# Thirty numbers in a list scheduler: new prices for matmuls, scans, strided views, half-array products, shape changes and hops between engines

## The chip, the cores and the metric

The kernel runs on one core of one Trainium2 chip. The metric is device time in microseconds (us) of one execution. The engines of the core are PE (TensorE, with PEld for its weight loads), DVE (VectorE), ACT (ScalarE), POOL (GpSimd) and SP (SyncE, which issues nearly all DMAs here).

## The reference

One layer of a hybrid decoder serves 2064 prompt tokens (16 of them learned meta tokens) and 64 sample tokens, 2128 columns in all. Cut to what matters:

```
q, k, v, u = split(rms_norm(x, g_mix) @ w_in)           # 1024 -> 512 | 128 | 128 | 512
o_att = sliding-window attention with sinks (8 query heads on 2 kv heads, window 128)
xr, xi = u_group @ Bbar                                 # 32 groups of 16 channels, 64 complex states each
h[t] = Lambda_bar * h[t-1] + x[t]                       # a scan over positions
y = Re(C h) + D u;  g = gelu(y);  o_ssm = g * sigmoid(g @ w_glu + b)
h = x + concat(rms_norm(o_att), rms_norm(o_ssm)) @ w_out
out = h + (silu(f @ w_gate) * (f @ w_up)) @ w_down,  f = rms_norm(h), 1024 -> 2816 -> 1024
```

It also returns the last 128 keys and values and the final scan states.

## The kernel before

All work is fp32. Large products are made from three products of fp32r halves (`mm3`), and the FFN uses a seven-product scheme on quarter matrices, so that the FFN is some 8300 matmuls of 352 columns. The program has five stages: `phase_u` (the projection to u, tiles `pu`, results `us` stored to `uD`), `phase_prep` (parameters of the scan), `phase_mix` (attention tiles of 128 tokens beside 16 scan steps of two channel groups each), `phase_out` (tiles `po`, after `out_weights` has split the output weights) and `phase_ffn` (tiles `ga`, `gb`, `gc`, `da`, `db`).

In `phase_mix` an attention tile is: `qkv_k` (48 matmuls into `pa`), `qk_sq`, `qk_n` (tile `qn`), `qkT`, `scores` (into `ps`, with the row maximum `mx` by a custom DVE instruction), exponentials on ACT, `p_t`, `p_v`. A scan step is: `ssm_x` (a product into `px`, then `xt` and `xs` on DVE), `ssm_add`, `ssm_scan` (two scans into `gg`), `ssm_rot` (`xt`, `xs` again), `ssm_h` (writes `hc`), `ssm_y` (products of `it` and of `mo` with `hc` into `yp`), `ssm_g`, `ssm_z` (a product into `px` again).

No line of these functions sets the order of the program. Every operation is recorded by `Plan.note` with its dependencies and with a price in ns from `Plan.price`. `Plan.issue` then plays a list schedule: each engine has a free time, an operation becomes ready when its producers have ended, plus a `hop` that depends on the two engines, and among the ready operations of an engine the one with the longest `tail` (priced work behind it, plus a bias per stage) goes next. PSUM banks are handed out in the same play. The operations are then emitted in the order of their played start times. Each engine runs its own instructions strictly in that order, and waits on semaphores for other engines' results and for its own earlier results. So a price has no effect on any instruction's duration; it decides what stands before what on each engine, and which bank a product uses.

Since every instruction is emitted by the recorder, all of them carry one source line in the profile (L279); tiles tell them apart.

Of the kernel before, what the change touches and what calls it, by code (L numbers as in the profile page):

```python
# [9 lines left out]
F32R = mybir.dt.float32r  # L10
# [160 lines left out]

class Op:
    __slots__ = ("eng", "cost", "wait", "call", "deps", "order", "next", "succ", "tail", "left", "ready", "start", "n", "set", "tiles",
                 "into", "part", "dma", "port")


class Plan:
# [18 lines left out]
    def turn(self, old, *new):  # L196

        pools = [LazyPool(self, *p) for p in new]

        def call():  # L200
            for p in [p for p in reversed(self.open) if p in old]:
                p.ctx.close()
                self.open.remove(p)
            for p in pools:
                p.ctx = ExitStack()
                p.got = p.ctx.enter_context(self.tc.tile_pool(name=p.name, bufs=p.bufs, side=p.side))
                self.open.append(p)

        if not old:
            call()  # L210
            return pools
        g = Op()
        g.eng, g.n, g.cost, g.wait, g.set, g.tiles, g.into = "gate", len(self.ops), 0, 0, None, [], None
        g.part = None
        g.order, g.dma, g.port = set(), False, False
        g.deps = set().union(*[p.ops for p in old])
        for p in old:
            p.over = True
        for p in pools:
            p.gate = g.n  # L220
        g.call = call
        self.ops.append(g)
        return pools

    def note(self, eng, name, args, kw):
        o = Op()
        o.eng, o.n, o.part = eng, len(self.ops), self.part
        vals = list(args) + list(kw.values())
        outs = [v for k, v in kw.items() if k in ("out", "accum_out")]
        if "out" not in kw:  # L230
            outs.append(args[0])
        outs = [v for v in outs if isinstance(v, Lazy)]
        ins = [v for v in vals if isinstance(v, Lazy) and not any(v is w for w in outs)]
        deps, order = set(), set()
        use = [(v.base, v.region(), False) for v in ins] + [(v.base, v.region(), True) for v in outs]
        for t, r, w in use:
            assert not t.over and not t.pool.over, t.kw
            if t.first is None:
                if t.pool.gate is not None:
                    deps.add(t.pool.gate)  # L240
                if t.before is not None:
                    t.before.over = True
                    deps.update(n for n, _ in t.before.reads + t.before.writes)
                if t.prev is not None and t.prev.first is not None:
                    order.add(t.prev.first)
            else:
                order.add(t.first)
            for n, rr in t.writes:
                if rr & r:
                    deps.add(n)  # L250
            if w:
# [12 lines left out]
        deps.discard(o.n)  # L264
        o.deps, o.order = deps, order - deps - {o.n}
        o.dma = "dma" in name
        o.cost, o.wait = self.price(eng, name, args, kw)
        o.port = self.ported(eng, name, outs, args, kw)
        fn = args[2] if eng == "scalar" and name == "activation" else None
        o.set = {AF.Sin: "sin", AF.Silu: "silu", AF.Exp: "exp", AF.Tanh: "exp"}.get(fn)  # L270

        bases = o.tiles = list({id(v.base): v.base for v in vals if isinstance(v, Lazy)}.values())
        o.into = next((v.base for v in outs if v.base.psum), None)
        for t in bases:
            t.count += 1

        def call():
            f = lambda v: v.real() if isinstance(v, Lazy) else v
            getattr(getattr(self.nc, eng), name)(*[f(v) for v in args], **{k: f(v) for k, v in kw.items()})  # L279
            for t in bases:  # L280
                t.count -= 1
                if not t.count:
                    t.got = None

        o.call = call
        self.ops.append(o)

    part, BIAS = None, {"prep": 3e3, "att": 6e3, **{"ssm%d" % i: 2e3 * (i - 4) for i in range(5, 17)}}

    HOP = {("tensor", "scalar"): 200, ("tensor", "vector"): 200, ("tensor", "gpsimd"): 225,  # L290
           ("vector", "tensor"): 256, ("vector", "scalar"): 200, ("vector", "gpsimd"): 205,
           ("scalar", "tensor"): 281, ("scalar", "vector"): 142, ("scalar", "gpsimd"): 170,
           ("gpsimd", "tensor"): 135, ("gpsimd", "vector"): 74, ("gpsimd", "scalar"): 75,
           ("tensor", "tensor"): 0, ("vector", "vector"): 127, ("scalar", "scalar"): 150, ("gpsimd", "gpsimd"): 102}

    def hop(self, a, b):
        if "gate" in (a, b):
            return 0
        if b == "sync":
            return 1250  # L300
        return 1100 if a == "sync" else self.HOP[a, b]

    PORT = False

    def ported(self, eng, name, outs, args, kw):

# [9 lines left out]
    def price(self, eng, name, args, kw):  # L316

        psum = lambda v: isinstance(v, Lazy) and v.base.psum
        out = kw.get("out", args[0] if args else None)
        n = int(np.prod(out.shape[1:]))  # L320
        ap = lambda v: isinstance(v, (Lazy, bass.AP))
        if "dma" in name:
            return 100 + out.shape[0] * n * 4 / (370 if out.shape[-1] >= 128 else 190), 1000
        if eng == "tensor":
            if name == "transpose":
                return 0.85 * args[1].shape[0], 0
            return (0.417 * n if args[1].dtype == F32R else 1.68 * max(n, 64)) + 3, 0
        if eng == "scalar":
            c = 0.83 * n + (60 if psum(args[1]) else 95) + 90 * ap(kw.get("bias")) + 90 * ap(kw.get("scale")) + 90 * ("accum_out" in kw)
            return c, 0  # L330
        if eng == "vector":
            if name == "tensor_reduce":
                return 1.04 * int(np.prod(args[1].shape[1:])) + 70, 0
            fast = name in ("tensor_copy", "tensor_scalar", "memset") and not psum(args[1] if len(args) > 1 else None)
            c = 65 + 65 * (name in ("tensor_scalar", "scalar_tensor_tensor") and ap(args[2]))
            return (3 if name == "reciprocal" else 0.52 if fast else 1.04) * n + c, 0
        if kw.get("op") == ALU.pow:
            return 165 * n + 300, 0
        return {"tensor_scalar": 1.37, "memset": 0.8, "tensor_copy": 1.0}.get(name, 2.15) * n + 135, 0

    def issue(self):
# [28 lines left out]
        banks = [(0.0, "b%d" % i) for i in range(8)]  # L370
        whole = {b: False for _, b in banks}
        left = {t: t.count for o in ops for t in o.tiles if t.psum}
        order, table, pipe, port = [], None, 0.0, 0.0
        for _ in ops:
            get = [min((b for b in banks if whole[b[1]] or not y), default=(1e12,)) for y in (False, True)]
            at = lambda o: (max(o.ready, get[o.into.seeded][0], 1e12 * bool(need.get(o.into))) if o.into and "tag" not in o.into.kw
                            else max(o.ready, port) if o.port and self.PORT else o.ready)
            free["sync"] = max(free["sync"], pipe)
            t, e = min((max(free[e], min(map(at, row))), e) for e, row in cand.items() if row)
            o = max((o for o in cand[e] if at(o) <= t), key=lambda o: o.tail)  # L380
# [10 lines left out]
            end = t + o.cost  # L391
            if o.dma:
                pipe = end = max(t + 2000 * (e == "gpsimd"), pipe) + o.cost
            if o.set is not None and o.set != table:
                end += 1283
                table = o.set
            free[e] = t + 1340 if o.dma and e == "gpsimd" else end
            if o.port:
                port = end
# [1378 lines left out]
```

## Time and profile before

| | |
|---|---|
| median of 3 runs | 2150.8 us (2147.27 to 2153.14) |
| profiled execution, its own time | 2150.36 us |
| span of the profile, first to last instruction | 2148.5 us |
| busy PE, DVE, ACT, POOL | 2049.7, 1735.1, 1295.8, 101.6 us |
| granted TensorE clock, mean | 0.977 of full speed |
| instructions | 35113 |

By the trace, the u projection ends on PE at about 148 us, the mix of attention and scan steps runs to about 570 us with output work beginning in it at 558 us, the output projection ends at about 785 us, and the rest is the FFN. Busy times of PE count the modelled end of each pipelined matmul, so they overstate; a matmul's cost in a dense stretch is read from the distance between starts.

### The profile page before, as it was taken

What the parts mean: (1) busy time and instruction counts of PE and PEld (TensorE: products, weight loads), DVE (VectorE), ACT (ScalarE), POOL (GpSimd) and SP (SyncE); (2) the same over time, 40 slices, a digit from 0 to 9 for tenths busy, and PEclk for the clock granted to TensorE, in tenths of its full rate; (3) what the DMA queues carried; (4) which work ended last, traced back from release to release, by engine and by line L of the source; (5) the groups of instructions that cost most, each with busy time, mean ns of one, the idle gap of its engine ahead of it and who ended that gap; (6) DMA issues with size and microseconds to landing.
All of it is one profiled execution on the core that took longest, in us unless ns stands there. A gap on an engine that the chain in (4) does not pass through costs nothing.

```text
span 2148.5 us, 35113 instructions
## 1 busy us (share of the span) xinstructions
PE 2049.7 (95%) x12625; PEld 1938.0 (90%) x12625; DVE 1735.1 (81%) x3688; ACT 1295.8 (60%) x2831; POOL 101.6 (5%) x97
## 2 busy tenths in 40 slices
PE   7989988898999999999999999999999999999998
PEld 7977766665898999999999899999999999999997
DVE  8776999987488769878788888878877987877876
ACT  6335766657444437566566756656656775665665
POOL 2001120112011000000000000000000000000000
PEclk9899999998899999999999999999999999999999
DMA  6673332224343645323322553332322722222222
GB/s 224 151 145 77 80 86 74 69 73 126 93 122 90 181 150 176 104 76 112 105 80 79 174 160 103 116 94 81 115 70 99 243 87 89 79 69 88 81 70 87
DMA packets 195150, 235.05 MB, mean 109 GB/s; under 512 B 54000, under 2 KB 155792, under 8 KB 194832
## 3 DMA queue, kind: packets, MB, share of 16 engines
q1 hardware_dynamic: 194976, 232.81, 36.3%
q8 instruction: 99, 1.62, 0.3%
q14 instruction: 75, 0.61, 0.1%
HBM read 187.92 MB, written 45.83 MB: 109 GB/s over the span
## 4 chain that ended last, share of the span: by engine, by line
PE 77%; DVE 14%; ACT 4%; DMA 3%; issue 1%; POOL 1%; SPq 0%; DVEq 0%; ACTq 0%
PE ga L279 23%; PE gc L279 12%; PE db L279 11%; PE da L279 8%; PE po L279 7%; PE gb L279 6%; PE pa L279 3%; PE pu L279 2%; PE ps L279 2%; DVE xs L279 2%; DVE xt L279 1%; DVE P L279 1%; PE pt L279 1%; PE yp L279 1%; ACT wb L279 1%
## 5 line engine op out<-in xcount | busy, mean ns | idle before, releaser
L279 PE MATMUL ga<-X,wb 128*128 128x352 f32 x3168 | 721.0, 324 | 7.0 <-ACT acc L279 2.9
L279 PEld LDWEIGHTS ga<-X,wb 128*128 128x128 f32 x3168 | 544.0, 188 | 10.9 <-ACT gb L279 3.8
L279 PE MATMUL gc<-X,wb 128*128 128x352 f32 x1584 | 401.6, 323 | 2.4 <-ACT acc L279 1.4
L279 PEld LDWEIGHTS gc<-X,wb 128*128 128x128 f32 x1584 | 278.7, 188 | 3.6 <-ACT acc L279 2.3
L279 ACT ACTIVATE wb<-S 128x512 fp32r<-128x512 f32 (+1 forms) x306 | 187.4, 617 | 154.3 <-PE ga L279 74.3
L279 DVE TENSOR_TENSOR wb<-S,wb 128x512 fp32r<-128x512 f32 (+1 forms) x306 | 203.5, 670 | 57.9 <-ACT wb L279 26.7
L279 ACT ACTIVATE wb<-r 128x512 fp32r<-128x512 f32 (+1 forms) x242 | 146.9, 613 | 124.9 <-PE gc L279 46.2
L279 PE MATMUL gb<-X,wb 128*128 128x352 f32 x792 | 216.7, 323 | 0.0
L279 PE MATMUL da<-wb 128*128 128x352 f32 x936 | 208.9, 323 | 3.2 <-DVE acc L279 1.6
L279 DVE TENSOR_TENSOR wb<-r,wb 128x512 fp32r<-128x512 f32 (+1 forms) x242 | 159.9, 668 | 51.6 <-PE gb L279 22.3
L279 PE MATMUL db<-wb 128*128 128x352 f32 x792 | 162.9, 323 | 4.4 <-ACT db L279 4.4
L279 PEld LDWEIGHTS da<-wb 128*128 128x128 f32 x936 | 159.4, 188 | 5.5 <-ACT wb L279 4.6
L279 PE MATMUL db<-gb,wb 128*128 128x352 f32 x792 | 161.0, 323 | 0.0
L279 ACT ACTIVATE wb<-fr 128x512 fp32r<-128x512 f32 (+1 forms) x166 | 101.9, 619 | 92.0 <-PE gc L279 40.1
L279 PE MATMUL pa<-wb,xh 128*128 128x512 f32 (+3 forms) x544 | 143.8, 357 | 0.3 <-DVE qn L279 0.3
L279 DVE TENSOR_TENSOR wb<-fr,wb 128x512 fp32r<-128x512 f32 (+1 forms) x166 | 110.8, 674 | 39.3 <-PE gb L279 16.0
L279 PEld LDWEIGHTS gb<-X,wb 128*128 128x128 f32 x792 | 142.2, 188 | 0.0
L279 PEld LDWEIGHTS db<-wb 128*128 128x128 f32 x792 | 132.7, 188 | 6.0 <-ACT db L279 6.0
L279 PEld LDWEIGHTS db<-gb,wb 128*128 128x128 f32 x792 | 133.1, 188 | 0.3 <-ACT db L279 0.3
L279 ACT ACTIVATE acc<-db 128x352 f32<-128x352 f32 x288 | 119.5, 457 | 20.7 <-PE db L279 19.9
L279 PE MATMUL po<-oh,wb 128*128 128x352 f32 x576 | 121.8, 335 | 2.1 <-ACT oh L279 1.5
L279 ACT ACTIVATE db<-acc 128x352 f32<-128x352 f32 x276 | 120.5, 465 | 2.4 <-DVE ru L279 2.2
(257 smaller groups left out, 3746.8 us busy)
## 6 DMA issues: line engine op xcount, KB each, us to landing
r<-w_up SPq DMA_DIRECT2D x41, 512.0 KB
r<-w_gate SPq DMA_DIRECT2D x38, 512.0 KB
r<-w_down SPq DMA_DIRECT2D x34, 512.0 KB
fr<-w_gate SPq DMA_DIRECT2D x28, 512.0 KB
fr<-w_down SPq DMA_DIRECT2D x26, 512.0 KB
fr<-w_up SPq DMA_DIRECT2D x25, 512.0 KB
acc<-xT SPq DMA_DIRECT2D x6, 1408.0 KB
hD<-acc SPq DMA_DIRECT2D x6, 1408.0 KB
```

The costliest lines, as they stand in the source:

```text
L279: getattr(getattr(self.nc, eng), name)(*[f(v) for v in args], **{k: f(v) for k, v in kw.items()})
```

## The change

The change edits only the tables from which the list schedule is played, and adds one: `geometry` names the part of the array that a product uses (all of it, 64 rows, or 64 columns), and a change of it costs the played PE 95 ns. A product of two fp32r operands costs 14 ns on top of its columns (before 3). A plain fp32 product on half of the array costs half. A scan costs 2.1 ns per element (before 1.04), the scores' custom instruction 1.08 n + 150, an ACT or DVE operation with an operand whose last dimension is strided 1.08 or 0.75 ns more per element. Most hops get shorter, and the hop from DVE to DVE and from ACT to ACT becomes 0. No recorded operation, tile or dependency changes.

```diff
-           ("vector", "tensor"): 256, ("vector", "scalar"): 200, ("vector", "gpsimd"): 205,
-           ("scalar", "tensor"): 281, ("scalar", "vector"): 142, ("scalar", "gpsimd"): 170,
+           ("vector", "tensor"): 190, ("vector", "scalar"): 118, ("vector", "gpsimd"): 165,
+           ("scalar", "tensor"): 200, ("scalar", "vector"): 132, ("scalar", "gpsimd"): 180,
-           ("tensor", "tensor"): 0, ("vector", "vector"): 127, ("scalar", "scalar"): 150, ("gpsimd", "gpsimd"): 102}
+           ("tensor", "tensor"): 0, ("vector", "vector"): 0, ("scalar", "scalar"): 0, ("gpsimd", "gpsimd"): 102}
...
-            return (0.417 * n if args[1].dtype == F32R else 1.68 * max(n, 64)) + 3, 0
+            if args[1].dtype == F32R:
+                return 0.417 * n + 14, 0
+            return 1.68 * max(n, 64) * (0.5 if self.geometry(args) != "full" else 1) + 6, 0
...
+            if name == "tensor_tensor_scan":
+                return 2.1 * n + 60, 0
+            if name == "tensor_tensor_reduce":
+                return 1.08 * n + 150, 0
+            return ((3 if name == "reciprocal" else 0.52 if fast else 1.05) + 0.75 * (slow > 0)) * n + c, 0
...
+            if o.geo != geo and o.geo:
+                end += 95
+                geo = o.geo
```

What this does to the program is seen in the order of instructions on each engine. Three places follow; `pu` is the u projection, `pa` the qkv projection, `pt` transposes, and `px`, `yp`, `hc`, `xt`, `xs`, `gg` belong to the scan steps as above.

On PE, at the end of the u projection, before:

```order
L279 MATMUL pu<-xh,wul 128x336 x3
L279 MATMUL pu<-xh,wuh 128x336 x3
L279 MATMUL pb<-idt,rx 128x128
L279 MATMUL pa<-wb,xl 128x512
L279 MATMUL pu<-xl,wuh 128x336 x3
L279 MATMUL pa<-wb,xh 128x512
L279 MATMUL pu<-xh,wul 128x336 x3
L279 MATMUL pa<-wb,xh 128x512
L279 MATMUL pa<-wb,xl 128x512
L279 MATMUL pa<-wb,xh 128x512 x2
```

And now:

```order
L280 MATMUL pu<-xh,wuh 128x336 x3
L280 MATMUL pu<-xl,wuh 128x336 x3
L280 MATMUL pu<-xh,wul 128x336 x3
L280 MATMUL pa<-wb,xh 128x512 x2
L280 MATMUL pa<-wb,xh 128x256 x2
```

The last u matmuls had qkv matmuls between them, and now the qkv projection begins only behind the last of them: 52 matmuls into `pa` stood ahead of the last one into `pu`, and now none does.

On PE, around the first scan step's products into `yp`, before:

```order
L279 MATMUL ps<-kT,qT 128x128 x16
L279 MATMUL pt<-idt,se 128x128 x4
L279 MATMUL pa<-wb,xh 128x512
L279 MATMUL pa<-wb,xl 128x512
L279 MATMUL pa<-wb,xh 128x512 x2
L279 MATMUL pa<-wb,xl 128x512
L279 MATMUL yp<-u,it 128x266 x2
L279 MATMUL pa<-wb,xh 128x512 x2
L279 MATMUL yp<-hc,mo 128x266 x2
L279 MATMUL pa<-wb,xl 128x512
```

And now:

```order
L280 MATMUL pa<-wb,xl 128x512
L280 MATMUL pa<-wb,xl 128x256
L280 MATMUL yp<-u,it 128x266 x2
L280 MATMUL yp<-hc,mo 128x266 x2
L280 MATMUL pa<-wb,xh 128x256 x2
L280 MATMUL pa<-wb,xl 128x256
L280 MATMUL pt<-idt,qn 128x128 x5
L280 MATMUL pa<-wb,xh 128x512 x2
L280 MATMUL pa<-wb,xl 128x512
```

This product has moved forward past two attention tiles' worth of work: ahead of it stand 93 matmuls into `pa` instead of 201.

On DVE, one scan step in the middle of the mix, before (the `ISA` rows are the scores' custom instruction and its accumulator read):

```order
L279 TENSOR_TENSOR xt<-xt,xs 128x516
L279 ISA P,mx<-ps,cst 128x256
L279 ISA mx 128x1
L279 SCALAR_TENSOR_TENSOR gg<-mag_1097,xt 128x258 x2
L279 ISA P,mx<-ps,cst 128x256
L279 ISA mx 128x1
L279 TENSOR_TENSOR xt<-gg,co 128x516
L279 TENSOR_TENSOR xs<-gg,si 64x516 x2
L279 ISA P,mx<-ps,cst 128x256
L279 ISA mx 128x1
L279 TENSOR_TENSOR hc<-xt,xs 128x2x257
```

And now:

```order
L280 TENSOR_TENSOR xt<-px,co 128x258
L280 TENSOR_TENSOR xs<-px,si 64x258 x2
L280 TENSOR_TENSOR xt<-xt,xs 128x516
L280 SCALAR_TENSOR_TENSOR gg<-mag_1215,xt 128x258 x2
L280 TENSOR_TENSOR xt<-gg,co 128x516
L280 TENSOR_TENSOR xs<-gg,si 64x516 x2
L280 TENSOR_TENSOR hc<-xt,xs 128x2x257
L280 TENSOR_TENSOR su<-su,ex 128x8
L280 RECIPROCAL su<-su 128x8
```

The chain of one step, each instruction reading what the one ahead of it wrote, had other work put between its links and now runs through without a break.

## Rows read from the trace of the kernel before

**Rows 1.** Windows: us, busy us (instructions) of PE, PEld, DVE, ACT, POOL, clock, DMA.

```profile
148.00:160.80 12.80, 7.36 (x44) 6.31 (x42) 10.33 (x20) 4.00 (x7) 0.55 (x2) 0.99 1.10 145
160.80:172.00 11.20, 7.71 (x33) 5.53 (x34) 9.92 (x29) 3.60 (x8) 4.51 (x5) 0.55 0.81 192
172.00:220.00 48.00, 48.00 (x343) 38.40 (x342) 27.46 (x106) 29.77 (x90) 5.92 (x7) 1.00 0.16 44
220.00:500.00 280.00, 250.74 (x1433) 183.78 (x1432) 256.09 (x693) 180.97 (x426) 40.35 (x48) 0.97 0.29 78
500.00:515.00 15.00, 15.00 (x101) 11.31 (x100) 9.54 (x32) 9.79 (x30) 1.95 (x1) 1.00 0.20 53
515.00:558.00 43.00, 31.17 (x227) 23.19 (x226) 34.84 (x105) 35.26 (x87) 10.57 (x8) 0.74 0.50 134
558.00:785.00 227.00, 218.62 (x1390) 213.23 (x1391) 148.96 (x312) 87.83 (x166) 18.80 (x14) 0.97 0.42 123
785.00:2148.50 1363.50, 1337.74 (x8289) 1328.01 (x8287) 1118.15 (x2102) 875.61 (x1907) 1.26 (x1) 1.00 0.34 107
1200.00:1260.00 60.00, 53.92 (x323) 51.43 (x323) 56.25 (x111) 44.76 (x103) 0.00 (x0) 1.00 0.74 240
1650.00:1710.00 60.00, 55.31 (x334) 53.16 (x333) 56.70 (x112) 46.95 (x107) 0.00 (x0) 1.00 0.67 212
```

**Rows 2.** Timeline of PE, 146 to 172: start, length, count, [idle before <-releaser].

```profile
155.08 0.28 PE L279 MATMUL pa<-wb,xl 128*128 128x256 f32 x1
160.85 2.11 PE L279 MATMUL px<-u,mi 128*128 128x266 f32 x4 [5.49 <-DVE t L279]
166.40 1.33 PE L279 MATMUL pt<-idt,qn 128*128 128x128 f32 x5 [3.43 <-DVE qn L279]
```

**Rows 3.** Timeline of SP, 146 to 172.

```profile
147.68 3.27 SPq L279 DMA_DIRECT2D uD<-us  x4
```

**Rows 4.** Timeline of DVE, 174 to 180.

```profile
176.87 0.36 DVE L279 TENSOR_SCALAR y<-cst,ph 128x258 f32<-128x258 f32 x1
177.14 0.69 DVE L279 TENSOR_TENSOR hc<-xt,xs 128x514 f32<-128x514 f32 x1
177.75 0.16 DVE L279 TENSOR_TENSOR fin<-xt,xs 128x2 f32<-128x2 f32 x1
177.82 0.35 DVE L279 TENSOR_SCALAR y<-cst,ph 128x258 f32<-128x258 f32 x1
178.20 0.70 DVE L279 TENSOR_SCALAR y<-y 128x1032 f32<-128x1032 f32 x1
```

**Rows 5.** The tile yp, 202 to 218: durations, first and last start.

```profile
L279 PE MATMUL yp<-hc,mo x4: 385/386/388, 203.0 to 203.7; 128*128 128x266 f32 x4
```

**Rows 6.** Waits of PE, 220 to 500: total us, times, longest.

```profile
PE yp L279 <- DVE hc L279: 10.0, 5, 2.7
PE px L279 <- DVE g L279: 4.0, 5, 1.1
```

**Rows 7.** Windows, 334.6 to 338.1, columns as in rows 1.

```profile
334.60:338.10 3.50, 3.50 (x18) 2.60 (x20) 3.05 (x9) 1.77 (x3) 0.55 (x3) 0.51 0.83 225
```

**Rows 8.** Timeline of PE, 331 to 340.

```profile
334.57 2.10 PE L279 MATMUL yp<-hc,mo 128*128 128x266 f32 x4 [2.02 <-DVE hc L279]
```

**Rows 9.** Timeline of DVE, 471 to 486.

```profile
476.10 1.27 DVE L279 TENSOR_TENSOR_SCAN gg<-mag,xt 128x258 f32<-128x258 f32 x2
477.29 0.79 DVE L279 TENSOR_REDUCE s<-sq 128x10 f32<-128x640 f32 x1
```

**Rows 10.** Timeline of ACT, 595 to 604.

```profile
601.67 0.84 ACT L279 ACTIVATE oh<-r 128x352 fp32r<-128x352 f32 x1 [0.26 <-DVE r L279]
602.41 0.49 ACT L279 ACTIVATE f<-r 128x352 f32<-128x352 f32 x1
```

**Rows 11.** Waits of PE, 558 to 785.

```profile
PE pr L279 <- DVE s L279: 3.9, 2, 3.6
PE po L279 <- ACT oh L279: 1.5, 3, 0.7
```

**Rows 12.** Waits of PE, 785 to 2148.

```profile
PE db L279 <- ACT db L279: 4.4, 5, 1.6
```

More of the change, by code (lines that the diff above doesn't have):

```diff
@@ L173 @@
     __slots__ = ("eng", "cost", "wait", "call", "deps", "order", "next", "succ", "tail", "left", "ready", "start", "n", "set", "tiles",
-                 "into", "part", "dma", "port")
+                 "into", "part", "dma", "port", "geo")
 class Plan:
@@ L214, in turn @@
         g.part = None
-        g.order, g.dma, g.port = set(), False, False
+        g.order, g.dma, g.port, g.geo = set(), False, False, None
         g.deps = set().union(*[p.ops for p in old])
@@ L268, in note @@
         o.port = self.ported(eng, name, outs, args, kw)
+        o.geo = self.geometry(args) if eng == "tensor" else None
         fn = args[2] if eng == "scalar" and name == "activation" else None
@@ L288 @@
     part, BIAS = None, {"prep": 3e3, "att": 6e3, **{"ssm%d" % i: 2e3 * (i - 4) for i in range(5, 17)}}
-    HOP = {("tensor", "scalar"): 200, ("tensor", "vector"): 200, ("tensor", "gpsimd"): 225,
-           ("vector", "tensor"): 256, ("vector", "scalar"): 200, ("vector", "gpsimd"): 205,
-           ("scalar", "tensor"): 281, ("scalar", "vector"): 142, ("scalar", "gpsimd"): 170,
+    HOP = {("tensor", "scalar"): 200, ("tensor", "vector"): 200, ("tensor", "gpsimd"): 275,
+           ("vector", "tensor"): 190, ("vector", "scalar"): 118, ("vector", "gpsimd"): 165,
+           ("scalar", "tensor"): 200, ("scalar", "vector"): 132, ("scalar", "gpsimd"): 180,
            ("gpsimd", "tensor"): 135, ("gpsimd", "vector"): 74, ("gpsimd", "scalar"): 75,
-           ("tensor", "tensor"): 0, ("vector", "vector"): 127, ("scalar", "scalar"): 150, ("gpsimd", "gpsimd"): 102}
+           ("tensor", "tensor"): 0, ("vector", "vector"): 0, ("scalar", "scalar"): 0, ("gpsimd", "gpsimd"): 102}
     def hop(self, a, b):
@@ L303, with geometry @@
     PORT = False
+    def geometry(self, args):
+        out, a = args[0], args[1]
+        rows = a.shape[0]
+        c = a.shape[1] if len(a.shape) > 1 else 1
+        return "rows" if rows == 64 else "cols" if out.shape[0] == 64 and c == 64 else "full"
     def ported(self, eng, name, outs, args, kw):
@@ L326, in price @@
                 return 0.85 * args[1].shape[0], 0
-            return (0.417 * n if args[1].dtype == F32R else 1.68 * max(n, 64)) + 3, 0
+            if args[1].dtype == F32R:
+                return 0.417 * n + 14, 0
+            return 1.68 * max(n, 64) * (0.5 if self.geometry(args) != "full" else 1) + 6, 0
+        slow = sum(isinstance(v, Lazy) and v.shape[-1] > 1 and v.idx.strides[-1] not in (0, v.idx.itemsize)
+                   for v in list(args) + list(kw.values()))
         if eng == "scalar":
-            c = 0.83 * n + (60 if psum(args[1]) else 95) + 90 * ap(kw.get("bias")) + 90 * ap(kw.get("scale")) + 90 * ("accum_out" in kw)
+            c = (0.83 + 1.08 * bool(slow) * (name == "activation")) * n + (60 if psum(args[1]) else 95) + 90 * ap(kw.get("bias")) + 90 * ap(kw.get("scale")) + 90 * ("accum_out" in kw)
             return c, 0
@@ L335, in price @@
             c = 65 + 65 * (name in ("tensor_scalar", "scalar_tensor_tensor") and ap(args[2]))
-            return (3 if name == "reciprocal" else 0.52 if fast else 1.04) * n + c, 0
+            if name == "tensor_tensor_scan":
[3 more added lines that the diff above has]
+            return ((3 if name == "reciprocal" else 0.52 if fast else 1.05) + 0.75 * (slow > 0)) * n + c, 0
         if kw.get("op") == ALU.pow:
@@ L372, in issue @@
         left = {t: t.count for o in ops for t in o.tiles if t.psum}
-        order, table, pipe, port = [], None, 0.0, 0.0
+        order, table, pipe, port, geo = [], None, 0.0, 0.0, None
         for _ in ops:
```

## The prediction

> **What bounds the kernel now.** I read the windows by stage first [rows 1]. From 785 us on PE is busy 1337.74 of 1363.50 us at a granted clock of 1.00, and 8289 matmuls in 1363.5 us are 164 ns each: the FFN is bound by PE. From 220 to 500 us DVE is busy 256.09 of 280 us (91%) while PE has gaps, and what PE waits for there is DVE: 10.0 us for `hc` and 4.0 us for the gate input `g` [rows 6]. So the settled part of the mix is bound by DVE. Between these lie stretches that nothing fills. From 172 to 220 PE has no gap at all, and DVE stands idle 20.5 of 48 us. From 515 to 558 PE is busy 31.17 of 43 us at a mean clock of 0.74, and DVE 34.84.
>
> Next I looked at the joints. At the first, the timeline of PE [rows 2] shows the last qkv matmul at 155.08, the first scan product `px` at 160.85 after 5.49 us of idleness, and a second wait of 3.43 us for `qn`. The stores of `us` are issued from 147.68 [rows 3]; `px` needs their readers, and everything of the new pools stands behind them, so the delay from the end of the u projection (about 147.9) to `px` is 13.0 us. The granted clock is 0.55 from 160.8 to 172 [rows 1].
>
> The second finding is how long a result can lie unused. `hc` of a first scan step starts at 177.14 and lasts 0.69 us [rows 4], but PE multiplies it only from 203.0 to 203.7 [rows 5]: 25 us in which PE works through attention tiles that stand ahead of it in its queue. That is the cause of DVE's idle 20.5 us: what scan work DVE could do is held up in PE's order.
>
> **The change part by part.** No instruction changes, so every term is one of waiting. Against the trace the new prices are mostly nearer: a 352-column matmul is priced 161 ns (before 150; measured 164 with the waits); two scans take 1.19 us from start to start, 0.595 each [rows 9], priced 0.60 (before 0.33); a strided `oh` takes 0.84 us and 0.74 to the next start, while a plain ACT copy of the same size lasts 0.49 [rows 10], priced 0.77 (before 0.39). One is further off, the hop from DVE to DVE (below).
>
> **Term 1, the first joint.** Before, 52 qkv matmuls stand ahead of the last u matmul, now none. 44 of them take 7.36 us [rows 1], 0.17 each, so u ends 52 x 0.17 = 9 us earlier, at about 139. The 13.0 us to `px` stay, so `px` comes at 152 instead of 160.85. Between them PE has 50 qkv matmuls, 8.4 us, so it idles some 4.5 us, and 46 more matmuls (8 us) then lie where it waited 3.43 us for `qn`. The scan loop starts 9 us earlier.
>
> **Term 2, the loop from `px` to the last qkv matmul.** Before, it runs from 160.8 to 515, 354 us, in which DVE is busy 9.92 + 27.46 + 256.09 + 9.54 = 303 us [rows 1] and idle 51. The first product with `hc` now stands behind 93 qkv matmuls instead of 201, so the 20.5 idle us of 172 to 220 can be filled: scan and attention advance together from the start. I assume that DVE idles throughout as it does from 220 to 500, 23.9 of 280 us, 8.5%. Against it stands a new cost. The hop of 0 lets a DVE instruction be placed right behind the one whose result it reads. In rows 4 the instruction behind an independent 258-column TENSOR_SCALAR starts 0.27 us after it (176.87 to 177.14), the dependent one behind the same shape 0.38 us after it (177.82 to 178.20): 0.11 us more. In the order I count 84 more such neighbours on DVE in this loop (486 against 126 in the whole program); some 25 of them follow a 64-row instruction, behind which even an independent one starts late, so 59 x 0.11 = 6.5, taken as 7 us. DVE then needs 303 + 7 = 310 us, and at 8.5% idleness the loop takes 339 us. The scan now ends with 81 qkv matmuls left instead of 40, a stretch with attention alone, for which I add 5 us (41 x 0.17 = 7 us of PE, mostly lost to DVE). So 344 us from 152: the last qkv matmul ends at 496 instead of 515, **-19 us**. Bounds: with the old idle share of the whole loop (51 of 303, 17%) it takes 362 us and ends at 514, -1; with 5% and no added stretch 326 us and 478, -37.
>
> **Term 3, the last attention tiles (515 to 558).** The same chain of scores, exponentials and transposes of two tiles and the sample stands there in both orders, as no output matmul can run before the split output weights. PE idles at least 12 us of it [rows 1], and either order could do better or worse by half of that: **0**, from -6 to +6.
>
> **Term 4, the output projection (558 to 785).** PE is bound, but waits 3.9 us for one `s` and 1.5 for `oh` [rows 11]. The old prices had the strided `oh` at half its length; the new one places the work ahead of it earlier. I take **-3** of these 5.4 us, from -8 to +4.
>
> **Term 5, the FFN.** PE waits little [rows 12]; the largest is 4.4 us for `db`. 206 of the new neighbours lie here, 206 x 0.11 = 23 us on DVE, which is busy 1118.15 of 1363.5 us [rows 1], so 245 us of idleness cover them. The cover is thin only in 1200 to 1260 and 1650 to 1710, where DVE is busy 56.25 and 56.70 of 60; I count 21 more neighbours in these two, 2.3 us. **0**, from -10 to +6.
>
> The 34 further changes of the array's shape on PE (162 against 128) fall in the mix, where PE waits for DVE anyway; without that cover they cost about 0.1 us each, 3 us, inside the bounds above.
>
> **Sum.** -19 + 0 - 3 + 0 = -22. Against the profiled execution's own 2150.4 us (span 2148.5 and 1.9 around it; the median of the runs, 2150.8, is practically the same) that is **2128 us**.
>
> **The rivals.** *Slower: the scan step's PE products become the bound of the loop.* In the new order `yp` follows its `hc` closely, and PE is strictly in order: a wait as at 334.57, 2.02 us for `hc` [rows 8], stops attention's matmuls too, and the clock is 0.51 in the 3.5 us behind it [rows 7], which cost 1.7 us. Today this happens in 5 of some 15 steps [rows 6]. In all 16 steps it would be 16 x 3.7 = 59 us of PE. It decides once DVE starves from it: the loop ends at 515 as now when DVE idles 14.6% of 363 us. With 18% it takes 378 us, the last qkv matmul ends at 530, +15, and the total is 2162. For it: attention starts with a lead of 93 matmuls instead of 201, so there is less to put between. Against it: the unbroken chain on DVE makes `hc` earlier.
>
> *No change: only the idleness moves.* The attention-only stretch behind the scan gives back what the start gains (term 2 at its upper bound, -1): 2145 to 2156. For it: PE work and DVE work are the same.
>
> *More gain:* term 2 at its lower bound, with terms 4 and 5 at half of theirs: -37 - 4 - 5 = -46, 2104.
>
> *Dependent neighbours cost nothing.* Then the 7 us of term 2 go, and the total is 2121. Rows 4 speak against it, with 0.38 against 0.27 us. The Trainium skill ("VectorE: DVE Perf Modes", section "The DRAIN you can't avoid") states this rival as its rule: chained DVE instructions with a semaphore behind each took as long as with one behind the last, so the semaphore costs nothing extra. By that rule the hop of 0 is right and the sum would be -29; the trace disagrees by its 0.11 us.
>
> **How the numbers follow.** Chances: forecast 0.50 (its own range 2112 to 2143), more gain 0.11, neighbours free 0.05, no change 0.16, slower 0.18. The predicted time is that of the forecast. The range of 2104 to 2158 leaves out part of the slower case and a little of the largest gain, some 2 in 10 together. A difference of 0.3%, 6.5 us, is about what a measurement of this kernel can tell from none. Faster by more: 0.50 + 0.11 + 0.05 = 0.66. Within: 0.16. Slower: 0.18.
>
> **What would show it.** Term 1: `px` first at about 152, PE's idleness before it under 5 us. Term 2: the first `yp` before 175, DVE busy over 85% from 172 to 220, the last qkv matmul near 496; DVE's busy stretches with TENSOR_SCALAR or RECIPROCAL 0.11 us behind their producers. Term 3: about 43 us from the last `pa` to the first `po`. Term 4: less than 5 us of waits of PE in the output projection. Term 5: an FFN of 1360 to 1365 us from its first `ga` to the end. The forecast is wrong if waits of `yp` for `hc` grow to more than 30 us in the mix, or if the stretch between the last scan step and the first `po` grows by more than what the start has gained.

## The result, and the profile after

The change made the kernel slower: 2173.0 us median (2171.4 to 2176.9) against 2152.0 us of the kernel before on the same chip, a ratio of 1.0104, with a 95% interval of 1.0083 to 1.0126. The forecast was 2128 us.

The windows of the changed kernel, cut at the first `px`, the last `pa`, the first `po` and the first `ga` (columns as in rows 1), with three shorter stretches:

```profile
133.80:149.60 15.80, 10.99 (x52) 8.81 (x50) 11.53 (x21) 3.97 (x4) 1.16 (x4) 0.89 1.09 141
149.60:509.80 360.20, 338.49 (x1976) 251.36 (x1976) 323.30 (x883) 235.54 (x573) 53.93 (x60) 0.98 0.31 83
509.80:541.10 31.30, 25.59 (x195) 18.35 (x193) 26.66 (x87) 23.90 (x66) 6.49 (x5) 0.74 0.36 110
541.10:782.40 241.30, 213.43 (x1359) 209.54 (x1359) 148.82 (x310) 88.61 (x164) 17.02 (x15) 0.93 0.38 113
782.40:2175.20 1392.80, 1363.62 (x8331) 1334.83 (x8329) 1133.42 (x2114) 882.02 (x1912) 1.25 (x1) 0.99 0.34 106
...
172.00:220.00 48.00, 48.00 (x291) 36.63 (x291) 45.48 (x135) 31.85 (x90) 6.13 (x8) 1.00 0.23 65
...
583.00:593.20 10.20, 5.68 (x23) 5.72 (x24) 7.59 (x15) 4.29 (x9) 1.35 (x1) 0.50 0.52 173
664.90:685.40 20.50, 7.33 (x29) 7.36 (x30) 15.54 (x32) 8.92 (x17) 1.00 (x1) 0.50 0.57 176
```

The cuts come from the tiles of the changed kernel (durations min/median/max in ns, first and last start):

```profile
L280 PE MATMUL px<-u,mi x64: 385/387/783, 149.6 to 464.0; 128*128 128x266 f32 x64
L280 PE MATMUL yp<-u,it x64: 385/388/812, 159.5 to 470.1; 128*128 128x266 f32 x64
L280 PE MATMUL yp<-hc,mo x64: 385/388/814, 160.5 to 472.4; 128*128 128x266 f32 x64
L280 PE MATMUL pa<-wb,xl x272: 276/388/796, 137.8 to 509.5; 128*128 128x512 f32 x65, 128*128 128x256 f32 x63, 128*80 128x512 f32 x4, 128*80 128x256 f32 x4
L280 PE MATMUL po<-oh,wb x576: 317/323/660, 541.1 to 780.0; 128*128 128x352 f32 x192
L280 PE MATMUL ga<-X,wb x3168: 317/323/642, 782.4 to 2136.4; 128*128 128x352 f32 x198
```

Set beside the same cuts of the kernel before (first `px` 160.9, first `po` 557.8, first `ga` 778.4, last matmul 2139.9), the balance of the two profiled executions (spans 2148.5 and 2175.2 us) is:

| stretch | before | after | difference |
|---|---|---|---|
| start to the first `px` | 160.9 | 149.6 | -11.3 |
| first `px` to first `po` (the mix) | 396.9 | 391.5 | -5.4 |
| first `po` to first `ga` (output projection) | 220.6 | 241.3 | +20.7 |
| first `ga` to the last matmul (FFN) | 1361.5 | 1383.7 | +22.2 |
| behind the last matmul | 8.6 | 9.0 | +0.4 |

So the mix and its start gained 17 us, nearly what was forecast for them, and two stretches whose terms were -3 and 0 lost 43. The medians differ by 21.0 us and these two executions by 26.7, so some 5 us of the balance are the scatter of single executions.

**The output projection.** The waits of PE between 541 and 785 us (total us, times, longest), and below them the waits of `yp` in the mix:

```profile
PE pq L280 <- DVE sa L280: 27.6, 4, 18.4
...
PE yp L280 <- DVE hc L280: 6.7, 5, 3.1
```

One kind of wait makes up the whole list: `pq<-one,sa`, which reads the serial sum of the norm's squares. Before, PE waited 5.4 us there for `s` and `oh` [rows 11], 1.4 us for other operands, and only once for `sa`:

```profile
PE pq L279 <- DVE sa L279: 1.4, 1, 1.4
```

The two long waits now, in the timeline of PE:

```profile
587.51 1.30 PE L280 MATMUL pq<-one,sa 128*88 128x1 f32 x8 [7.63 <-DVE sa L280]
...
655.77 0.47 PE L280 MATMUL pr<-idt,s 88*128 88x88 f32 x4
678.07 1.30 PE L280 MATMUL pq<-one,sa 128*88 128x1 f32 x8 [18.44 <-DVE sa L280]
```

And in the timeline of DVE, ahead of the second of them:

```profile
666.36 1.83 DVE L280 TENSOR_TENSOR X<-acc,X 128x352 fp32r<-128x352 f32 x4
668.10 2.68 DVE L280 TENSOR_TENSOR acc<-acc,po 128x352 f32<-128x352 f32 x6
670.68 1.83 DVE L280 TENSOR_TENSOR X<-f,X 128x352 fp32r<-128x352 f32 x4
672.42 0.79 DVE L280 TENSOR_TENSOR r<-r,pr 128x352 f32<-128x352 f32 x1
673.12 0.52 DVE L280 TENSOR_TENSOR sa<-f 128x352 f32<-128x352 f32 x1
673.75 1.16 DVE L280 TENSOR_TENSOR sa<-sa,f 128x352 f32<-128x352 f32 x2
674.82 0.79 DVE L280 TENSOR_TENSOR r<-r,pr 128x352 f32<-128x352 f32 x1
675.51 2.42 DVE L280 TENSOR_TENSOR sa<-sa,f 128x352 f32<-128x352 f32 x4
677.84 1.47 DVE L280 TENSOR_TENSOR ol<-r,oh 128x352 fp32r<-128x352 f32 x2
```

DVE does not stop in these lines, so this is no idle engine but an order. The six sums `acc<-acc,po` that release the output tiles are done at about 670.8 us, and the tiles of the next projection that wait behind `pq` have all but the last two of their eight pairs of `oh` and `ol` by then. But `pq` stands ahead of them in PE's queue, and its sum comes last on DVE, at 677.9. The granted clock is 0.50 from 664.9 to 685.4, so the matmuls behind the wait are slow as well.

In PE's order this can be counted. Matmuls into `po` that stand ahead of the sums `pq` of the first three token tiles' norms: 241, 422 and 646 before, 192, 414 and 576 now (the expectations below count 16 more in each place, in every order alike). One token tile is 192 such matmuls, so 192 and 576 are the places at which the next tile has to be opened. At 0.16 us each, 49 and 70 of them, 8 and 11 us of work, have moved behind a wait of 7.6 and one of 18.4 us.

**The FFN.** No wait of that length stands there, and the listed waits grew little. The windows show the loss in a stretch with no visible idleness, 900 to 1100 us, first of the changed kernel, then of the kernel before:

```profile
900.00:1100.00 200.00, 199.80 (x1226) 195.59 (x1225) 160.97 (x294) 125.37 (x271) 0.00 (x0) 1.00 0.32 101
```

```profile
900.00:1100.00 200.00, 200.00 (x1248) 199.47 (x1247) 165.09 (x305) 127.01 (x273) 0.00 (x0) 1.00 0.32 101
```

PE counts as busy in both, but does 22 matmuls less, and PEld is busy 195.6 us for 199.5. I therefore took the distances between the starts of neighbouring matmuls: over the FFN 81 of them were between 0.18 and 1 us before, 258 now, and what they exceed 165 ns by sums to 11.3 and 31.8 us. That is 20.5 of the 22.2 us lost. (12 and 31 of them lie where the granted clock was below full; they hold 1.5 and 4.2 us of the two sums.) A distance is not yet a wait: the 258 lie in 172 groups, 56 of them pairs of a late matmul and the one behind it. One such pair in the timeline of the changed kernel (PE, PEld and DVE):

```profile
992.78 0.52 DVE L280 TENSOR_TENSOR acc<-acc,da 128x352 f32<-128x352 f32 x1
992.85 0.19 PEld L280 LDWEIGHTS db<-wb 128*128 128x128 f32 x1
993.01 0.32 PE L280 MATMUL db<-wb 128*128 128x352 f32 x1
...
993.35 0.46 PEld L280 LDWEIGHTS da<-wb 128*128 128x128 f32 x3 [0.30 <-DVE acc L280]
993.35 0.75 PE L280 MATMUL da<-wb 128*128 128x352 f32 x3
```

The product `da` needs `acc<-acc,da`, which ends at 993.30. It starts 0.34 us after the matmul ahead of it instead of 0.16, and its weights are loaded only then, not under the matmul ahead. The next matmul comes 0.265 us behind it instead of 0.16, so a wait of 0.18 us costs 0.28.

The 28 waits of this kind that the trace shows in the FFN to end on DVE, and 27 that end on ACT, put a number on the hop into PE. The scheduler prices a DVE operation by its distance to the next one, so its priced end lies some 80 to 100 ns ahead of the end in the trace. From the priced end, the waiting matmul starts 136 ns later (median; ACT 148), and the one behind it comes as if its predecessor had started 242 ns later (ACT 258). The old prices were 256 and 281, the new ones 190 and 200.

### The profile page after: what moved, and what is told of

Read it like the earlier page. It is cut to its first block, busy times and chain, and to the rows that moved or that the text cites. A ratio compares the mean times of both kernels' runs of the same rounds, so it can differ in the third digit from the quotient of the medians.

```text
span 2175.2 us, 35120 instructions
## 1 busy us (share of the span) xinstructions
PE 2070.4 (95%) x12625; PEld 1938.2 (89%) x12625; DVE 1753.9 (81%) x3688; ACT 1297.8 (60%) x2829; POOL 97.1 (4%) x97
## 4 chain that ended last, share of the span: by engine, by line
PE 77%; DVE 14%; ACT 3%; issue 3%; DMA 2%; POOL 1%; SPq 0%; DVEq 0%; ACTq 0%; POOLq 0%
PE ga L280 22%; PE gc L280 10%; PE db L280 10%; PE da L280 8%; PE po L280 7%; PE gb L280 6%; PE pa L280 4%; PE pu L280 3%; PE ps L280 3%; DVE wb L280 2%; DVE xs L280 1%; PE pt L280 1%; DVE acc L280 1%; DVE xt L280 1%; PE px L280 1%
## 5 line engine op out<-in xcount | busy, mean ns | idle before, releaser
L280 PE MATMUL ga<-X,wb 128*128 128x352 f32 x3168 | 759.0, 326 | 10.1 <-ACT gb L280 7.3
L280 PE MATMUL gc<-X,wb 128*128 128x352 f32 x1584 | 423.0, 324 | 1.6 <-ACT acc L280 1.3
L280 PE MATMUL gb<-X,wb 128*128 128x352 f32 x792 | 231.3, 323 | 0.0
L280 PE MATMUL da<-wb 128*128 128x352 f32 x936 | 217.4, 326 | 3.0 <-ACT wb L280 1.8
L280 PE MATMUL db<-wb 128*128 128x352 f32 x792 | 170.9, 328 | 4.5 <-ACT db L280 4.5
L280 PE MATMUL db<-gb,wb 128*128 128x352 f32 x792 | 165.7, 324 | 0.1
L280 PE MATMUL pa<-wb,xh 128*128 128x256 f32 (+3 forms) x544 | 147.5, 362 | 1.2 <-DVE mx L280 1.2
```

## The experiments

Unless it says otherwise, each kernel is the changed kernel with the one edit shown. All were timed against the kernel before on the chip on which they ran. The stretches are those of the balance above, each from its run's own trace, so from one execution; the whole times of one kernel's executions lie 1 to 16 us apart. "Small" counts the distances between matmul starts of 0.18 to 1 us in the FFN.

| run | us, median | ratio to before (95%) | px to po | output | FFN | small |
|---|---|---|---|---|---|---|
| before | 2152 to 2153 | 1 | 396.9 | 220.6 | 1361.5 | 81 |
| the change | 2173.0 | 1.0104 (1.0083 to 1.0126) | 391.5 | 241.3 | 1383.7 | 258 |
| e1_same_engine | 2135.4 | 0.9919 (0.9896 to 0.9941) | 391.0 | 215.5 | 1371.3 | 180 |
| e2_all_hops | 2134.2 | 0.9909 (0.9889 to 0.9929) | 401.6 | 216.3 | 1362.0 | 103 |
| e3_old_spacing | 2165.7 | 1.0055 (1.0035 to 1.0076) | 392.6 | 249.9 | 1365.5 | 99 |
| e4_hops_into_pe | 2152.8 | 0.9997 (0.9985 to 1.0008) | 385.5 | 235.1 | 1372.4 | 183 |
| e5_sum_chain | 2156.8 | 1.0017 (1.0007 to 1.0026) | 397.5 | 217.2 | 1381.7 | 238 |
| e6_same_and_pe | 2125.3 | 0.9863 (0.9849 to 0.9878) | 386.8 | 214.6 | 1362.6 | 99 |
| e7_before_same0 | 2171.5 | 1.0085 (1.0065 to 1.0104) | 397.5 | 244.6 | 1356.9 | 75 |
| e8_spacing_13 | 2171.3 | 1.0078 (1.0063 to 1.0093) | 408.6 | 229.6 | 1377.9 | 235 |
| e9_no_half_price | 2147.5 | 0.9979 (0.9964 to 0.9993) | 387.2 | 219.1 | 1360.8 | 101 |
| e10_no_scan_price | 2120.9 | 0.9851 (0.9813 to 0.9890) | 377.9 | 218.0 | 1363.9 | 106 |
| e11_hops_pe_125 | 2171.8 | 1.0098 (1.0069 to 1.0127) | 391.6 | 232.4 | 1384.7 | 326 |
| e12_with_old_spacing | 2128.3 | 0.9885 (0.9854 to 0.9915) | 389.8 | 227.9 | 1355.0 | 65 |

**First: which price loses which stretch.** Each of four runs takes one part of the change back.

```diff
-           ("tensor", "tensor"): 0, ("vector", "vector"): 0, ("scalar", "scalar"): 0, ("gpsimd", "gpsimd"): 102}
+           ("tensor", "tensor"): 0, ("vector", "vector"): 127, ("scalar", "scalar"): 150, ("gpsimd", "gpsimd"): 102}
```

> The changed kernel, with the hops within VectorE and within ScalarE set back to 127 and 150 ns. Three theories of the 21 us lost. (A) The hop of 0 within an engine is the cause: dependent neighbours cost 0.11 us each, and the serial sums of the norm are priced too short, so PE stands 18.4 and 7.6 us before pq in the output projection; then the output projection (first po to first ga) falls from 241 to about 222 us, the FFN from 1384 to about 1370, and the total to about 2140. (B) The exact matmul spacing is the cause in the FFN: the output projection falls to about 222, the FFN stays at 1380 to 1388, total about 2154. (C) Any change of prices shuffles the order and moves each stage by 10 to 20 us without a pattern: all stages move, none to its value of before.

Measured: output projection 215.5, FFN 1371.3, total 2135.4, near the 222, 1370 and 2140 of theory A. B fails on the FFN, which moved though the spacing stayed.

The second run takes back the whole table of hops:

```diff
-    HOP = {("tensor", "scalar"): 200, ("tensor", "vector"): 200, ("tensor", "gpsimd"): 275,
-           ("vector", "tensor"): 190, ("vector", "scalar"): 118, ("vector", "gpsimd"): 165,
-           ("scalar", "tensor"): 200, ("scalar", "vector"): 132, ("scalar", "gpsimd"): 180,
+    HOP = {("tensor", "scalar"): 200, ("tensor", "vector"): 200, ("tensor", "gpsimd"): 225,
+           ("vector", "tensor"): 256, ("vector", "scalar"): 200, ("vector", "gpsimd"): 205,
+           ("scalar", "tensor"): 281, ("scalar", "vector"): 142, ("scalar", "gpsimd"): 170,
...
-           ("tensor", "tensor"): 0, ("vector", "vector"): 0, ("scalar", "scalar"): 0, ("gpsimd", "gpsimd"): 102}
+           ("tensor", "tensor"): 0, ("vector", "vector"): 127, ("scalar", "scalar"): 150, ("gpsimd", "gpsimd"): 102}
```

> The changed kernel with the whole table of hops of before, those into PE included (256 and 281 ns for 190 and 200). If the small waits of PE in the FFN come from hops into PE that are priced too short (theory D), the FFN falls to 1362 to 1368 us here and not in the run with only the same-engine hops restored, and the total comes to about 2130. By theory B (matmul spacing) the FFN stays at 1380 or more, total 2150 or more. By theory A it comes out as the run with the same-engine hops alone, within 5 us.

Measured: FFN 1362.0, the value of before. So the hops explain the whole of its loss with the matmul at its exact price; the total of 2134.2 is 4 above what was expected, because the mix took 401.6.

```diff
-                return 0.417 * n + 14, 0
+                return 0.417 * n + 3, 0
```

> The changed kernel with the fp32r matmul priced at 0.417 n + 3 ns as before (150 ns for 352 columns where the trace has 160). Theory B: a price that is too short makes the planner place the operands of PE earlier than PE really comes to them; with the exact price they arrive just in time, and each small delay costs PE a weight load that could not be prefetched. Then the FFN falls from 1384 to about 1362 us here, and the small waits vanish; the output projection keeps its 18 us wait; total about 2152. Theories A and D: the FFN stays within 5 us of 1384, total 2165 to 2180.

Measured: FFN 1365.5 with 99 small waits instead of 258. That is near theory B's number too. B and D then fit one account: a reserve, which either longer hops or too cheap matmuls give. The output projection did not stay but grew to 249.9, with 34.9 us of waits for `sa`, and the total missed by 14 us.

```diff
-           ("vector", "tensor"): 190, ("vector", "scalar"): 118, ("vector", "gpsimd"): 165,
-           ("scalar", "tensor"): 200, ("scalar", "vector"): 132, ("scalar", "gpsimd"): 180,
+           ("vector", "tensor"): 256, ("vector", "scalar"): 118, ("vector", "gpsimd"): 165,
+           ("scalar", "tensor"): 281, ("scalar", "vector"): 132, ("scalar", "gpsimd"): 180,
```

> The changed kernel with only the hops from VectorE and ScalarE into PE set back to 256 and 281 ns. Theory D: the FFN falls to about 1365 us, the output projection stays near 241, total about 2155. Theories A and B: FFN stays within 5 us of 1384, and so does the total with 2173.

Measured: FFN 1372.4, half of the loss, where theory D expected nearly all of it (1365). With e1 (1371.3) and e2 (1362.0) the hops into PE and within an engine come out as about equal shares.

**Second: the race of `pq`, alone and in the old kernel.** If the output projection is lost by one position in PE's order, a delay on one kind of instruction must give it back.

```diff
+            sums = 127 if name == "tensor_add" and out.base.kw["name"] == "sa" else 0
-            return ((3 if name == "reciprocal" else 0.52 if fast else 1.05) + 0.75 * (slow > 0)) * n + c, 0
+            return ((3 if name == "reciprocal" else 0.52 if fast else 1.05) + 0.75 * (slow > 0)) * n + c, sums
```

> The changed kernel, with a delay of 127 ns put back for one kind of instruction alone: the additions of the norm's serial sum (sa). All other neighbours on VectorE keep the hop of 0. In PE's order the multiplications pq that read this sum stand behind 257, 438 and 662 output matmuls before the change, behind 208, 430 and 592 with it, and here behind 261, 445 and 669. Theory A1 (the hop of 0 costs through this one race in the list schedule, pq ahead of the output matmuls that could run): the output projection falls from 241 to 214 to 222 us, the waits of pq for sa from 27.6 to under 3 us, the FFN stays at 1384 within 4 us, total 2144 to 2156. Theory A2 (it costs through dependent neighbours all over VectorE, 0.11 us each): the output projection stays above 232, total above 2162.

Measured: output projection 217.2, FFN 1381.7. PE's waits between 547 and 765 us are now:

```profile
PE po L280 <- DVE ol L280: 5.4, 1, 5.4
PE pr L280 <- DVE s L280: 1.9, 3, 0.8
```

`pq` is gone from them. For the output projection A2 is ruled out: the other dependent neighbours still have the hop of 0. The total is 1 us above the range, since the mix took 6 us more.

The kernel before, with the hops within an engine alone set to 0:

```diff
-           ("tensor", "tensor"): 0, ("vector", "vector"): 127, ("scalar", "scalar"): 150, ("gpsimd", "gpsimd"): 102}
+           ("tensor", "tensor"): 0, ("vector", "vector"): 0, ("scalar", "scalar"): 0, ("gpsimd", "gpsimd"): 102}
```

> The kernel before, with one part of the change alone: the hops within VectorE and within ScalarE set to 0. pq stands behind 208, 432 and 592 output matmuls, as in the changed kernel. Theory A1: the output projection rises from 220.6 to 234 to 244 us with waits of pq for sa of 15 us or more; the FFN stays below 1366 us, because its matmuls are still priced 150 ns; total 2163 to 2180. Theory C (shuffling): stages move without this pattern.

Measured: output projection 244.6, FFN 1356.9, total 2171.5; and the waits of PE from 561 to 806 us show the same line:

```profile
PE pq L279 <- DVE sa L279: 27.9, 4, 18.4
```

So these two zeros alone make the old kernel 0.85% slower. The FFN, whose matmuls are still priced 150 ns here, is not harmed by them (1356.9 for 1361.5).

**Third: both hops together, and a control.**

```diff
-           ("vector", "tensor"): 190, ("vector", "scalar"): 118, ("vector", "gpsimd"): 165,
-           ("scalar", "tensor"): 200, ("scalar", "vector"): 132, ("scalar", "gpsimd"): 180,
+           ("vector", "tensor"): 256, ("vector", "scalar"): 118, ("vector", "gpsimd"): 165,
+           ("scalar", "tensor"): 281, ("scalar", "vector"): 132, ("scalar", "gpsimd"): 180,
...
-           ("tensor", "tensor"): 0, ("vector", "vector"): 0, ("scalar", "scalar"): 0, ("gpsimd", "gpsimd"): 102}
+           ("tensor", "tensor"): 0, ("vector", "vector"): 127, ("scalar", "scalar"): 150, ("gpsimd", "gpsimd"): 102}
```

> The changed kernel with both hops that helped apart: within an engine 127 and 150, into PE 256 and 281 ns; the hops between VectorE and ScalarE stay at the new values. If the FFN's small waits come from how late PE's operands are planned, and the two add up, the FFN comes to 1360 to 1365 us as with the whole old table, the output projection to 214 to 222, the total to 2124 to 2135. If the hops between VectorE and ScalarE (118 for 200 ns) matter as well, the FFN stays above 1367.

Measured: 1362.6, 214.6 and 2125.3, 1.4% under the kernel before. The windows of this run (output projection, FFN, and the quiet stretch) show PE at 1241 matmuls in 200 us, where the change had 1226, and the clock of the output projection back at 0.98:

```profile
538.10:752.60 214.50, 208.82 (x1358) 205.51 (x1358) 143.37 (x303) 87.04 (x162) 20.20 (x15) 0.98 0.43 127
752.60:2123.50 1370.90, 1345.24 (x8331) 1332.69 (x8329) 1115.77 (x2114) 878.48 (x1912) 2.11 (x1) 1.00 0.35 108
900.00:1100.00 200.00, 199.45 (x1241) 198.48 (x1240) 157.93 (x292) 124.06 (x264) 0.00 (x0) 1.00 0.30 89
```

The control moves one price by 1 ns:

```diff
-                return 0.417 * n + 14, 0
+                return 0.417 * n + 13, 0
```

> A control for how much the smallest change of a price moves: the changed kernel with the fp32r matmul priced 1 ns less (0.417 n + 13). pq stands behind 238, 430 and 592 output matmuls, so the second long wait stays (18 us) and the first goes. If the stages follow the mechanisms named, the output projection is 230 to 236 us and the FFN 1378 to 1386 us. By theory C (any change of prices shuffles) the FFN moves by 10 us or more either way. The mix is left open: its last part is a chain that differs from order to order by some 10 us in the runs so far (31 to 47 us from the last pa to the first po).

Measured: output projection 229.6 with one wait of 18.4 us left, FFN 1377.9, both within a microsecond of what the mechanisms say. The mix took 17 us more. That is the scatter of the mix for a change that means nothing, and no difference of the mix below it is explained here.

**Fourth: what the rest of the change is worth.** These start from e6.

```diff
-            return 1.68 * max(n, 64) * (0.5 if self.geometry(args) != "full" else 1) + 6, 0
+            return 1.68 * max(n, 64) * (1) + 6, 0
```

> The kernel of the run with both hops restored (2125 us), with the half price of the half-array products taken back. It is the price that could move the start of the mix: without it 96 qkv matmuls stand ahead of the first px and 192 ahead of the first yp, with it 62 and 96. Theory M1 (the early start of the mix, px at 150 for 161 and yp at 155 to 160 for 202, comes from this price alone): px 157 to 164 us, yp 190 to 206, first po 549 to 560, output projection and FFN as before within 4 us (215 and 1363), total 2136 to 2148. Theory M2 (it comes from the scans, the strided views or the price of a shape change): px and yp stay within 6 us of 151 and 160, total 2120 to 2130.

Measured: total 2147.5. The tiles:

```profile
L280 PE MATMUL px<-u,mi x64: 385/387/782, 168.2 to 493.1; 128*128 128x266 f32 x64
L280 PE MATMUL yp<-u,it x64: 385/388/814, 200.9 to 499.2; 128*128 128x266 f32 x64
```

`px` at 168.2 is even later than forecast, `yp` at 200.9 as before the change. The early start of the mix needs this one price (M1; that it needs no other one is not shown, since the old kernel with this price alone was not run): in all eleven kernels that have it `px` comes between 144 and 152 us, in the three without it (before, e7, e9) between 161 and 168. At the first `po` it is worth 17 us here (555.4 for 538.1), all of it from the earlier `px`; from `px` to `po` the two kernels take the same (387.2 and 386.8).

```diff
-            if name == "tensor_tensor_scan":
-                return 2.1 * n + 60, 0
-            if name == "tensor_tensor_reduce":
-                return 1.08 * n + 150, 0
+            if name == "tensor_tensor_scan":
+                return 1.05 * n + c, 0
+            if name == "tensor_tensor_reduce":
+                return 1.05 * n + c, 0
```

> The kernel of the run with both hops restored (2125 us), with the prices of the scan and of tensor_tensor_reduce taken back (0.33 and 0.43 us where the trace has 0.595 for a scan). If the nearer price is worth something in the mix, the time from px to the first po rises from 387 to 395 us or more and the total to 2132 or more. If the order of the mix holds without it, the total stays within 6 us of 2125. Output projection and FFN 215 and 1363 within 4 us.

Measured: the mix took 377.9 instead of 386.8, not more, and the interval of the ratio (0.981 to 0.989) takes in e6's 0.986. Of the new prices this one came nearest to the trace, and it gains nothing that shows.

```diff
-           ("vector", "tensor"): 190, ("vector", "scalar"): 118, ("vector", "gpsimd"): 165,
-           ("scalar", "tensor"): 200, ("scalar", "vector"): 132, ("scalar", "gpsimd"): 180,
+           ("vector", "tensor"): 125, ("vector", "scalar"): 118, ("vector", "gpsimd"): 165,
+           ("scalar", "tensor"): 125, ("scalar", "vector"): 132, ("scalar", "gpsimd"): 180,
```

(This one starts from the changed kernel.)

> The opposite of the runs that restored it: the changed kernel with the hops from VectorE and ScalarE into PE lowered further, from 190 and 200 to 125 ns. Theory D (a hop into PE that is priced too short plans PE's operands just in time, and every small delay costs PE about 0.1 us and more): the small waits of PE in the FFN grow from 258 to 330 or more and the FFN from 1384 to 1392 to 1404 us. If the price does not matter, the FFN stays within 4 us of 1384. The output projection stays at 228 to 244 (pq behind 238, 430 and 592 output matmuls).

Measured: 326 small waits, but the FFN at 1384.7 and their excess at 31.5 us, as with 190. Theory D said 1392 or more: the harm does not grow below 190. More waits, each shorter; why they trade off so evenly I did not settle.

```diff
-                return 0.417 * n + 14, 0
+                return 0.417 * n + 3, 0
```

> Both hops restored as in the run of 2125 us, and the fp32r matmul at its old price of 150 ns as well: more reserve for PE's operands. If reserve still pays, the FFN falls below 1360 us (1357 in the run of the kernel before with the hops of 0 alone); the third and fourth pq stand behind 674 and 784 output matmuls (661 and 842 in the run of 2125), so one wait of pq may return: output projection 214 to 228. Total 2118 to 2135. If the hops had already given all there was, the FFN stays at 1361 to 1365.

Measured: FFN 1355.0 with 65 small waits, the best of all, and an output projection of 227.9 with 5.2 us of `pq` waits for `sa` again, as its order said, and longer waits for other operands beside them. In sum it is no better than e6.

## Why the prediction was wrong, step by step

**The steps that failed are terms 4 and 5**, -3 and 0 in the forecast, +20.7 and +22.2 in the trace. Both looked at what a new price describes and not at what it does to the order.

*Term 4, output projection.* I costed a nearer price for `oh` and gave it 3 of 5.4 us (the 3.9 us for `s` were two waits, not one). What decided was the hop of 0: the serial sum of seven additions is played almost 1 us shorter, so `pq` becomes ready in the play just ahead of the moment at which the next output tile may be opened (that needs all its operands placed), and PE's queue gets `pq` first. By the play's own count it was half a microsecond at the long wait (`pq` ready at 607.06 us of played time, the tile's last `ol` placed at 607.57) and 2.6 us at the other (523.32 and 525.90). On the chip it costs 24 us between e5 and the change. The matmuls ahead of `pq` could be read from the order before the run; of the three places that I set side by side, none lay in this stretch. The play itself shows the loss, too: in it PE stands idle for 6.7 and 17.5 us ahead of these two `pq` (measured 7.6 and 18.4), and in the plays of the kernel before and of e5 ahead of no `pq` of this norm.

*Term 5, FFN.* I asked whether DVE has cover for 206 dependent neighbours, 23 us, and found 245 us of idleness. The cover was the wrong question. PE is the bound there, and what it needs is operands that are early; the old table gave this by a matmul 10 ns too cheap and by hops of 127 to 281 ns. The change corrects the first, which was an error, and cuts the second, which by the waits above was hardly one: 256 and 281 ns into PE were priced where the trace has 242 and 258. Either alone would have cost nothing or little (e2 1362.0, e3 1365.5, e7 1356.9), both together cost 22 us. That this is nearly the 23 us of the neighbours is chance: e3 and e7 have the same zeros and FFNs of 1365.5 and 1356.9. The shorter hops into PE (256 to 190, 281 to 200) I never costed at all.

*Term 1* was right in kind: `px` first at 149.6, forecast 152. PE's idleness ahead of it is 4.8 of 15.8 us, forecast below 5.

*Term 2* had the right sum from two wrong halves with the next term. `yp` starts at 159.5 (forecast before 175), DVE is busy 45.48 of 48 us from 172 to 220 (95%, forecast over 85%). But the last `pa` came at 509.8, not 496. DVE's idle share was 10.2% where I took 8.5%; the failing number is the work. I carried 303 us over from the old loop, and the new one holds 323.3 and 883 instructions for 857. The windows on both sides of the loop, ahead of the first `px` and behind the last `pa` before, and ahead of the first `px` now, say where they came from:

```profile
0.00:160.90 160.90, 140.74 (x820) 134.61 (x820) 130.23 (x314) 73.02 (x122) 18.33 (x16) 0.92 0.68 173
515.30:557.80 42.50, 30.67 (x224) 22.69 (x222) 34.70 (x104) 34.96 (x87) 10.50 (x8) 0.74 0.50 134
...
0.00:149.60 149.60, 129.25 (x774) 124.17 (x774) 121.75 (x296) 67.72 (x115) 18.41 (x16) 0.94 0.76 180
```

DVE does 8.5 us less ahead of `px` and, with 26.66 us there now, 8.0 less behind the last `pa`: 16.5 of the 20.3 us have moved into the loop. The earlier start moves work, it does not remove it. Dependent neighbours add about what I said: from the start to the first `po` DVE is busy 471.7 us in the change against 464.0 in e1, and 472.1 in e7 against 467.9 before, 4 to 8 us, forecast 7.

*Term 3* was 0, and was -11 (31.3 us from the last `pa` to the first `po`, for 42.5): the shorter end, whose work had moved into the loop, makes good what term 2 lacks, so that the mix ended at 541 where the sum says 539. Since the 1 ns control moved the mix by 17 us, I count neither as understood.

*The rivals.* The slower one that I had put its 0.18 on, PE's products as the bound of the loop, did not happen: PE's waits of `yp` for `hc` were 6.7 us, not above 30. That the sign came out on its side is no credit to it. The rival of free neighbours falls again, by a better row than rows 4: four dependent `sa<-sa,f` take 677.84 - 675.51 = 2.33 us, 0.583 each, six independent `acc<-acc,po` of the same size 670.68 - 668.10 = 2.58, 0.43 each. The difference is 0.15 us. The Trainium skill ("VectorE: DVE Perf Modes", section "The DRAIN you can't avoid") says that eight DVE copies with a semaphore behind each took as long as with one behind the last, so that the semaphore costs nothing extra; it does not say that those copies read one another's results, and where the adds here do, this trace has those 0.15 us more. The old hop of 127 ns was the better price.

## What to carry to other kernels

The prices of a list schedule are not only forecasts of time: they set how early operands lie ready, and a price that makes the bounding engine look faster, or a hop longer, is a reserve. Correct such a price only while another reserve stands, as the old hops did in e2, or put one in by name, and look for its loss in the distances between starts of the bounding engine, since a wait of 0.1 us shows as busy time. When a table changes, read in the new play where the bounding engine stands idle, and count in the new order what stands ahead of every instruction that reads the end of a serial chain on another engine: an in-order engine pays for a race of half a microsecond with everything queued behind it. And a gain at a joint is worth only what the next stretch has idle on all its engines, for the work that filled the joint comes along.

## What the runs showed of the hardware

A late operand costs PE more than its lateness. Behind a matmul that waited, the next one came 0.265 us later instead of 0.16, because the weights were not loaded under the matmul ahead (at 993.35 the load starts with its matmul); the 55 waits measured add 0.105 us each in the median. A planner's hop from DVE to PE would by this be 0.24 us behind the priced end, not the 0.136 us at which the waiting matmul starts. That is an estimate from these waits: e4 and e6, with 256 and 281 ns, bear it out, but e11, where 125 ns did no more harm than 190 and 200, does not.

The FFN of the runs follows the count of the small distances: with 65 of them it takes 1355 us, with 99 1362.6 (e6) and 1365.5 (e3), with 180 1371.3, with 258 1383.7, about 0.15 us for each. The others lie within 6 us of this line, and only e11 leaves it, with 326 and 1384.7 where the line has 1394.
